# lora_A over ScalarE's queue in sixteen transfers instead of one over SyncE's

## The chip, the cores and the metric

The kernel runs on one core of one Trainium2 chip. The time is device microseconds of that core for one execution; the median of the runs is compared. The profile is of one execution, taken by the hardware profiler; its span runs from the first to the last instruction, and the execution's own time is somewhat longer than the span.

## The reference

A linear layer with a low-rank addition whose rank directions are scaled:

```
x_flat = x.reshape(-1, 256)                    # x: 16 x 2048 x 256, so 32768 rows
y = x_flat @ W                                 # W: 256 x 256
lora_out = ((x_flat @ lora_A) * lora_E) @ lora_B     # A: 256 x 16, E: 16, B: 16 x 256
out = y + scale * lora_out                     # scale = 1.0, all float32
```

## The kernel before

The kernel does not carry the low-rank path along with the data. It folds it into the weight once, at the start: weff = W + A diag(E) scale B, in bfloat16. Then each row of the output is one product of x with weff. To do this, PE transposes the two halves of lora_A (`a_sb`, L280) against an identity that POOL makes (L149 to L154), DVE scales the transposed A by `e_sb` into `ate` (L227), POOL casts `b_sb` to `b_bf` (L156), PE multiplies the two (L284), and DVE adds `w_sb` and writes `weff` (L233).

The 32768 rows are worked through in 32 steps of 8 x 128 rows. The transfers go in 11 chunks (`PLAN`), ten of three steps (3 MB each) and one of two (2 MB). SBUF has four buffers of three steps each, shared by inputs and outputs; `X_AT` and `Y_AT` say which chunk goes to which buffer. A chunk's load waits until every step of the chunk that used its buffer has been transposed (L128): loads 0 to 3 have a fresh buffer, load 4 waits for the six steps of chunks 0 and 1, load 5 for nine steps, and so on. All stores stand behind all loads on SyncE's queue, and the first store waits for the last load but one (L143).

A step goes through these stages. DVE rounds x to bfloat16 (`xb`, L198). PE transposes it as pairs of bfloat16 in float32 clothing into PSUM (`ps_xt`, L258). DVE or ACT copies that to `xt`, where up to 22 steps are kept (L188). DVE moves it to `xm` (L211). PE multiplies it by weff (L267) into `ps_y`, and ACT or DVE copies the result to the output buffer (L180). The order of DVE's work is written out by hand in `VECTOR`: r is a rounding, t a transposed step, m a move, y a result. In it, the making of `ate` and of `weff` stands right after `r0`, so that every later rounding stands behind it on DVE. The order on PE is set by `FIRST` and `SECOND`: the products of the first steps begin when six or seven rounds of transposes have been done, and the making of the low-rank product stands ahead of all transposes of x.

The transfers that concern the change are issued at L131 to L137, all by SyncE: W, chunk 0 of x, lora_A, lora_B, lora_E, then the other chunks. lora_A, lora_B and lora_E share the semaphore `s_l`, on which each adds 16, and three engines wait until it stands at 48 before they begin the low-rank path: POOL at L155, DVE at L225 and PE at L277.

ScalarE (ACT) issues no transfer. Its first instructions are the load of its activation table and then the copy of step 1's transposes (L188).

Of the kernel before, what the change touches and what calls it, by code (L numbers as in the profile page):

```python
# [20 lines left out]

FIRST = [6, 7, *range(14, 28)]
SECOND = [6, *range(13, 28)]


VECTOR = """
# [8 lines left out]
def kernel(  # L35
# [20 lines left out]
    KC = K // P  # L56
    H = S // Q
    CHUNKS, STEPS = len(PLAN), sum(PLAN)
    ROUNDS = max(*FIRST, *SECOND) + 1
    assert len(FIRST) + len(SECOND) == STEPS  # L60
    assert K == M == KC * P and STEPS * S * P == N

    def sbuf(name, shape, dt):
        return ctx.enter_context(nc.sbuf_tensor(name, shape, dt))
# [11 lines left out]
    a_sb = sbuf("a_sb", [P, KC, R], FP32)  # L76
# [15 lines left out]
    s_l = sem("s_l")  # L92
# [28 lines left out]
    with tc.tile_critical(sync_engine=mybir.EngineType.SP, no_gpsimd_drain=True):  # L121
        sp, pe, dve, act, pool = nc.sync, nc.tensor, nc.vector, nc.scalar, nc.gpsimd


        def load(i):
            if x_before[i] is not None:

                sp.wait_ge(s_t, first[x_before[i]] + PLAN[x_before[i]])  # L128
            sp.dma_start(out=rows_at(X_AT[i], 0, PLAN[i] * S), in_=rows_of(x_flat, i)).then_inc(s_io[i], 16)

        sp.dma_start(out=w_sb[:], in_=W.rearrange("(p c) m -> p c m", c=KC)).then_inc(s_w, 16)  # L131
        load(0)
        sp.dma_start(out=a_sb[:], in_=lora_A.rearrange("(p c) r -> p c r", c=KC)).then_inc(s_l, 16)
        sp.dma_start(out=b_sb[:], in_=lora_B).then_inc(s_l, 16)
        sp.dma_start(out=e_sb[:], in_=lora_E[:, None]).then_inc(s_l, 16)
        for i in range(1, CHUNKS):
# [8 lines left out]
        for i in range(CHUNKS - 3):  # L145
# [6 lines left out]
            out=ident[:], in_=ident[:], compare_op=mybir.AluOpType.not_equal, fill=1.0,  # L152
            base=0, pattern=[[-1, P]], channel_multiplier=1,
        ).then_inc(s_id, 1)  # L154
        pool.wait_ge(s_l, 48)  # L155
        pool.tensor_copy(out=b_bf[:], in_=b_sb[:]).then_inc(s_lora, 1)  # L156


# [15 lines left out]
        def y_of(q, engine, copy):  # L174
            k, h = q // H, q % H
            i = chunk[k]
            if y_before[i] is not None:
                ensure(engine, s_io[y_before[i]], 32)
            ensure(engine, s_p, q + 1)
            done = copy(out=rows_at(Y_AT[i], (k - first[i]) * S + h * Q, Q), in_=ps_y[h][:])  # L180
            last = k == first[i] + PLAN[i] - 1
            done.then_inc(s_rdy[h] if last else s_y[h], 1)

        def transposes_of(k, engine, copy):
            ensure(engine, s_t, k + 1)
            if k >= KEPT:
                ensure(engine, s_mv, k - KEPT + 1)
            copy(  # L188
                out=xt[:, k % KEPT].rearrange("w j p c -> w j (p c)"), in_=ps_xt[k % 2][:].bitcast(BF16),
            ).then_inc(s_c[k % 2], 1)  # L190


        def round_step(k):
            i = chunk[k]
            ensure(dve, s_io[i], 16)
            if k >= 2:
                ensure(dve, s_t, k - 1)
            dve.tensor_copy(  # L198
                out=xb[k % 2][:], in_=rows_at(X_AT[i], (k - first[i]) * S, S),
            ).then_inc(s_xb, 1)  # L200

        def move(k):


            if k + 2 < STEPS:
                ensure(dve, s_t, k + 3)
            else:
                dve.wait_ge(s_c[k % 2], 1)
            if k >= 2:
                ensure(dve, s_p, (k - 1) * H)  # L210
            dve.tensor_copy(out=xm[k % 2][:], in_=xt[:, k % KEPT]).then_inc(s_mv, 1)  # L211

        vectors = set(VECTOR.split())
        for what in VECTOR.split():
            n = int(what[1:])
            if what[0] == "r":
                round_step(n)
            elif what[0] == "t":
                transposes_of(n, dve, dve.tensor_copy)
            elif what[0] == "m":  # L220
                move(n)
            else:
                y_of(n, dve, dve.tensor_copy)
            if what == "r0":
                dve.wait_ge(s_l, 48)  # L225
                dve.wait_ge(s_lpe, 1)
                dve.tensor_scalar(  # L227
                    out=ate[:], in0=ps_at, scalar1=e_sb[:], scalar2=float(scale),
                    op0=mybir.AluOpType.mult, op1=mybir.AluOpType.mult,
                ).then_inc(s_lora, 1)  # L230
                dve.wait_ge(s_w, 16)
                dve.wait_ge(s_lpe, 2)
                dve.tensor_add(out=weff[:], in0=w_sb[:], in1=ps_aeb).then_inc(s_lora, 1)  # L233


        def rounds():
            k = 0
            for n in range(ROUNDS):
                for b, these in enumerate((FIRST, SECOND)):
                    if n in these:  # L240
# [33 lines left out]
            pe.sem_inc(s_y[h], 1)  # L274
        for b in range(2):
            pe.sem_inc(s_c[b], 1)
        pe.wait_ge(s_l, 48)  # L277
        pe.wait_ge(s_id, 2)
        for c in range(KC):
            t = pe.transpose(ps_at[:, c, :], a_sb[:, c, :], ident[:])  # L280
# [7 lines left out]

        bits = [sum(1 << n for n in these) for these in (FIRST, SECOND)]
        with pe.Fori(0, ROUNDS) as n:  # L290
# [45 lines left out]
```

## Time and profile before

| | |
|---|---|
| median of 2 runs | 166.51 us (166.48 to 166.55) |
| profiled execution | 166.21 us |
| its span | 164.4 us |
| busy, PE / DVE / ACT / POOL | 103.4 / 99.9 / 72.1 / 1.6 us |
| moved | 67.43 MB, mean 410 GB/s |
| issue to landing: W / lora_A / lora_B / lora_E | 2.7 / 9.4 / 9.2 / 9.4 us |
| mean granted clock of TensorE | 0.91 |

The page divides the span into 40 slices of some 4.1 us, with one digit of busy share each (9 is 90% or more). Engines are PE (TensorE), PEld (its weight loads), DVE (VectorE), ACT (ScalarE), POOL (GpSimd) and SP (SyncE); SPq is SyncE's own queue of transfers. q1 and q14 are queues of the sixteen DMA engines: q1 carries the kernel's transfers, q14 the fetching of instructions. A line of a timeline gives start, duration, engine, line of the code, operation, destination and source, and in brackets how long the engine had been idle and what ended that. A line of the waits gives who waited for whom, the sum, how often, and the longest.

### The profile page before, as it was taken

The numbers are of one execution on the slowest core, as the hardware profiler recorded it, in microseconds if no ns is written. First come the engines' busy times: TensorE is split into PE (matmuls) and PEld (weight loads), VectorE is DVE, ScalarE is ACT, GpSimd is POOL, SyncE is SP. The second block draws the span as 40 slices with busy tenths as digits, with TensorE's granted clock in tenths as the row PEclk, the third lists the DMA queues.
The fourth block names the chain that finished last, engine by engine and source line by source line (L and its number), as shares of the span: only waits on it lengthen the run. The fifth ranks groups of instructions, "written<-read, shape, count | busy, mean of one in ns | idle before, by whom it ended". The sixth has DMA issues, their size and how long they took to land. (4 is left out here: it accounts for less than half of the span.)

```text
span 164.4 us, 2431 instructions
## 1 busy us (share of the span) xinstructions
PE 103.4 (63%) x772; PEld 82.0 (50%) x772; DVE 99.9 (61%) x101; ACT 72.1 (44%) x62; POOL 1.6 (1%) x7
## 2 busy tenths in 40 slices
PE   0003763858884567966799887878878787880000
PEld 0001652747674447745699665655666565560000
DVE  0016699786969496787999765667466466730000
ACT  3000254146796413441477665446546544652000
POOL 1002000000000000000000000000000000000000
PEclk9999999599999675599999999999999999999555
DMA  5999999999999999999999999999999999999970
GB/s 165 460 403 460 401 460 401 460 401 460 401 466 395 466 395 466 395 466 385 420 460 401 454 407 460 413 442 424 436 424 436 424 432 424 442 424 430 426 301 12
DMA packets 3523, 67.43 MB, mean 410 GB/s; under 512 B 560, under 2 KB 576, under 8 KB 704
## 3 DMA queue, kind: packets, MB, share of 16 engines
q1 hardware_dynamic: 3520, 67.41, 96.2%
q14 instruction: 3, 0.02, 0.0%
HBM read 33.85 MB, written 33.55 MB: 410 GB/s over the span
## 5 line engine op out<-in xcount | busy, mean ns | idle before, releaser
L267 PE MATMUL ps_y<-weff,xm 128*128 128x256 bf16 x512 | 62.8, 272 | 9.9 <-PEq L264 8.8
L180 ACT COPY xy<-ps_y 128x1024 f32<-128x1024 f32 x49 | 48.7, 1016 | 35.2 <-PE ps_y L267 34.5
L267 PEld LDWEIGHTS ps_y<-weff,xm 128*128 128x128 bf16 x512 | 47.3, 97 | 24.3 <-issue 19.2
L258 PE MATMUL ps_xt<-ident,xb 128*128 128x128 f32 x256 | 41.4, 319 | 21.9 <-PEq L256 21.8
L198 DVE CAST xb<-xy 128x2048 bf16<-128x2048 f32 x32 | 38.6, 1221 | 23.7 <-DMA xy<-in_x_dram 20.2
L258 PEld LDWEIGHTS ps_xt<-ident,xb 128*128 128x128 f32 x256 | 34.7, 165 | 28.2 <-issue 28.1
L188 ACT COPY xt<-ps_xt 128x2048 bf16<-128x2048 bf16 x12 | 22.4, 1868 | 41.1 <-PE ps_xt L258 41.1
L180 DVE COPY xy<-ps_y 128x1024 f32<-128x1024 f32 x15 | 18.4, 1225 | 17.2 <-PE ps_y L267 17.2
L188 DVE COPY xt<-ps_xt 128x2048 bf16<-128x2048 bf16 x20 | 24.2, 1216 | 1.0 <-PE ps_xt L258 0.9
L211 DVE COPY xm<-xt 128x2048 bf16<-128x2048 bf16 x32 | 21.8, 685 | 4.4 <-PE ps_y L267 4.4
L280 PE MATMUL ps_y<-ident,a_sb 128*16 128x128 f32 x2 | 0.6, 402 | 12.2 <-DMA e_sb<-in_lora_E_dram 12.2
L280 PEld LDWEIGHTS ps_y<-ident,a_sb 128*16 128x16 f32 x2 | 0.1, 94 | 12.2 <-DMA e_sb<-in_lora_E_dram 12.2
L188 ACT ACT_TABLE_LOAD x1 | 1.3, 1283 | 0.9 <-SPq L121 0.9
L233 DVE TENSOR_TENSOR weff<-w_sb,ps_y 128x512 bf16<-128x512 f32 x1 | 0.7, 687 | 0.8 <-PE ps_y L284 0.8
L156 POOL CAST b_bf<-b_sb 16x256 bf16<-16x256 f32 x1 | 0.9, 912 | 10.6 <-DMA e_sb<-in_lora_E_dram 10.6
L284 PE MATMUL ps_y<-b_bf,ate 16*128 16x256 bf16 x2 | 0.6, 404 | 0.6 <-DVE ate L227 0.6
L284 PEld LDWEIGHTS ps_y<-b_bf,ate 16*128 16x128 bf16 x2 | 0.1, 106 | 1.1 <-DVE ate L227 1.1
L227 DVE TENSOR_SCALAR ate<-ps_y,e_sb 16x256 bf16<-16x256 f32 x1 | 0.5, 472 | 0.0
L151 POOL TENSOR_SCALAR_AFFINE_SELECT ident<-ident 128x128 f32<-128x128 f32 x1 | 0.3, 294 | 0.2 <-POOL ident L149 0.2
L149 POOL MEMSET ident<- 128x128 f32 x1 | 0.2, 205 | 0.5 <-SPq L121 0.5
L317 POOL MEMSET const-bfloat16-1.0<- 128x1 bf16 x1 | 0.1, 103 | 0.0
L317 POOL MEMSET const-uint8-127<- 128x1 uint8 x1 | 0.1, 102 | 0.0
(2 smaller groups left out, 0.2 us busy)
## 6 DMA issues: line engine op xcount, KB each, us to landing
xy<-in_x_dram SPq DMA_DIRECT2D x10, 3072.0 KB, 14.4
out_dram<-xy SPq DMA_DIRECT2D x10, 3072.0 KB, 12.5
xy<-in_x_dram SPq DMA_DIRECT2D x1, 2048.0 KB, 12.7
out_dram<-xy SPq DMA_DIRECT2D x1, 2048.0 KB, 13.7
w_sb<-in_W_dram SPq DMA_DIRECT2D x1, 256.0 KB, 2.7
a_sb<-in_lora_A_dram SPq DMA_DIRECT2D x1, 16.0 KB, 9.4
b_sb<-in_lora_B_dram SPq DMA_DIRECT2D x1, 16.0 KB, 9.2
e_sb<-in_lora_E_dram SPq DMA_DIRECT2D x1, 0.1 KB, 9.4
```

The source lines that it names most:

```text
L151: pool.affine_select(out=ident[:], in_=ident[:], compare_op=mybir.AluOpType.not_equal, fill=1.0, base=0, pattern=[[-1, P]], channel_multip ...
L156: pool.tensor_copy(out=b_bf[:], in_=b_sb[:]).then_inc(s_lora, 1)
L180: done = copy(out=rows_at(Y_AT[i], (k - first[i]) * S + h * Q, Q), in_=ps_y[h][:])
L188: copy(out=xt[:, k % KEPT].rearrange("w j p c -> w j (p c)"), in_=ps_xt[k % 2][:].bitcast(BF16),).then_inc(s_c[k % 2], 1)
L198: dve.tensor_copy(out=xb[k % 2][:], in_=rows_at(X_AT[i], (k - first[i]) * S, S),).then_inc(s_xb, 1)
L211: dve.tensor_copy(out=xm[k % 2][:], in_=xt[:, k % KEPT]).then_inc(s_mv, 1)
L227: dve.tensor_scalar(out=ate[:], in0=ps_at, scalar1=e_sb[:], scalar2=float(scale), op0=mybir.AluOpType.mult, op1=mybir.AluOpType.mult,).the ...
L233: dve.tensor_add(out=weff[:], in0=w_sb[:], in1=ps_aeb).then_inc(s_lora, 1)
L258: t = pe.transpose(ps_xt[b][:, j, :], xb[b][:, j, :].bitcast(FP32), ident[:])
L267: m = pe.matmul(ps_y[h][:, j, :], xm[b][:, h * Q + j, :, c], weff[:, c, :], start=(c == 0), stop=(c == KC - 1),)
L280: t = pe.transpose(ps_at[:, c, :], a_sb[:, c, :], ident[:])
L284: m = pe.matmul(ps_aeb[:, c, :], ate[:, c, :], b_bf[:], start=True, stop=True)
```

## The change

lora_A's 128 partitions are no longer loaded by one transfer of SyncE's queue that stands behind chunk 0, but by sixteen transfers that ScalarE issues, of 15, 14, 13 and so on down to 1 partitions and one of 8. They are ScalarE's first instructions, ahead of its table load. Each adds 16 to `s_l`, so the three waits ask for (16 + 2) x 16 = 288. The bytes moved are the same, and so are all other instructions and their order on each engine. In the diff, `p` runs over the partitions.

```diff
+A_PIECES = [*range(15, 0, -1), 8]
...
         load(0)
-        sp.dma_start(out=a_sb[:], in_=lora_A.rearrange("(p c) r -> p c r", c=KC)).then_inc(s_l, 16)
+
+        p = 0
+        for n in A_PIECES:
+            act.dma_start(
+                out=a_sb[p:p + n], in_=lora_A.rearrange("(p c) r -> p c r", c=KC)[p:p + n],
+            ).then_inc(s_l, 16)
+            p += n
         sp.dma_start(out=b_sb[:], in_=lora_B).then_inc(s_l, 16)
...
-        pool.wait_ge(s_l, 48)
+        pool.wait_ge(s_l, (len(A_PIECES) + 2) * 16)
...
-                dve.wait_ge(s_l, 48)
+                dve.wait_ge(s_l, (len(A_PIECES) + 2) * 16)
...
-        pe.wait_ge(s_l, 48)
+        pe.wait_ge(s_l, (len(A_PIECES) + 2) * 16)
```

## The prediction

> **What bounds the kernel now.** I read the page's slices and queues first, then the waits and SP's part of the timeline, then the first 16 us of the timeline, then the trace's own records of DMA packets (one for each packet, with start, duration and size).
>
> The transfers are the bound. In the slices, the DMA row stands at 9 from slice 1 to slice 37, and section 3 gives one queue 96.2% of sixteen engines' span; the stages say the same:
>
> ```profile
> DMA  5999999999999999999999999999999999999970
> q1 hardware_dynamic: 3520, 67.41, 96.2%
> ```
>
> ```profile
> 20.00:33.00 13.00, 7.71 (x48) 6.50 (x48) 11.94 (x12) 5.61 (x4) 0.00 (x0) 0.87 0.99 425
> 33.00:82.00 49.00, 34.73 (x240) 29.09 (x241) 39.05 (x37) 24.24 (x18) 0.00 (x0) 0.86 1.00 427
> 82.00:150.00 68.00, 56.50 (x466) 43.11 (x464) 43.38 (x49) 40.34 (x41) 0.00 (x0) 1.00 1.01 432
> ```
>
> (Columns: stretch, length, busy PE, PEld, DVE, ACT, POOL, granted clock, DMA share, GB/s.) The reader is to see a DMA share of 0.99 to 1.01 in every stage, with DVE at 80% or less after 33 us. So a change costs time only where it makes the sixteen engines idle or gives one of them more work, and gains only by the opposite.
>
> The second thing to read is where they could be made idle. Loads 4 to 10 reuse buffers and wait for transposes:
>
> ```profile
> SPq L140 <- ACT xy L180: 67.7, 10, 8.0
> SPq L129 <- PE ps_xt L258: 63.4, 7, 21.7
> SPq L331 <- DMA out_dram<-xy: 12.5, 1, 12.5
> ```
>
> The longest of the seven waits, 21.7 us, is that of load 4, which waits for six steps of transposes; three lines of the timeline show how they come to start:
>
> ```profile
> 2.80 0.55 SPq L135 DMA_DIRECT2D e_sb<-in_lora_E_dram  x1
> 3.39 1.42 SPq L129 DMA_DIRECT2D xy<-in_x_dram  x3
> 11.68 1.23 DVE L198 CAST xb<-xy 128x2048 bf16<-128x2048 f32 x1 [11.68 <-DMA xy<-in_x_dram]
> 12.23 0.60 PE L280 MATMUL ps_y<-ident,a_sb 128*16 128x128 f32 x2 [12.23 <-DMA e_sb<-in_lora_E_dram]
> ...
> 14.79 1.22 DVE L198 CAST xb<-xy 128x2048 bf16<-128x2048 f32 x1
> ```
>
> ```profile
> 26.54 0.33 SPq L129 DMA_DIRECT2D xy<-in_x_dram  x1
> ```
>
> PE, DVE and POOL all stand at the low-rank semaphore until 12.19 us, when the last increment of e_sb lands. I call that moment L. Load 4 is issued at 26.54, so 14.35 us after L, and the work between (rounding, transposes, evictions) waits for no load. Loads 0 to 3 keep the engines busy meanwhile: chunk 3's increments land from 32.98 to 33.71, and a last packet ends some 0.3 us before its increment, so the engines run dry at about 32.8. A load's first packet starts 1.0 us after its issue (W: issued at 0.95, first packet at 1.96). Load 4 may therefore be issued as late as 31.8, and L may slip from 12.2 to about 17.5 us before one engine idles. Past that, each microsecond of L is a microsecond of the run: all that follows is transfers end to end.
>
> **The change, part by part.** *SP gives up one issue* (0.42 us and a gap of 0.04): b_sb, e_sb and loads 1 to 3 are issued 0.46 us sooner. That gains nothing, as they stand behind chunk 0 on the engines: e_sb, issued at 2.80, landed at 12.19. The 128 packets of a_sb leave that queue: 8 a engine of 13 ns and one semaphore packet of 9 ns, 0.11 us. If e_sb still ended the wait, L would be 12.1: hidden under the 5.3 us of slack.
>
> *ACT gets sixteen issues.* No row shows ACT issuing; SP's take 0.33 to 0.55 us, so 5.3 to 8.8 us, and I take 0.45 with the gap, 7.2 us: from 0.95 (where the table load starts now) to 8.1, then the table load, 1.28 us, to 9.4. Cover: ACT's first copy starts at 19.41 after 17.2 us of idleness. Even 1 us an issue would be hidden; without the cover each would delay that copy by itself.
>
> *The three waits* ask for 288 instead of 48; they wait for the same data. Behind them stand, on PE every transpose, on DVE every rounding after the first, on POOL the cast of b_sb and the passing on of semaphores. If the pieces are late, all of it is.
>
> *Packets.* The data are the same 128 packets of 128 bytes. Before, each of 26 transfers put 16 semaphore packets of 4 bytes on the engines (432 such records, 16 of them e_sb's data). A piece of n partitions has at most n shares: 128 semaphore packets against 16. The busiest engine gets at least 8 data packets (an even spread) and at most one from each piece if every transfer starts over at the same engine, 16. No row shows which. Nearest is that in all later stores one and the same engine falls further behind (last landing 0.5 us behind the next in the fourth store, 2.4 us in the last), as if every transfer was cut over the engines alike; so I take 16. The Trainium skill (DMA: Bandwidth & Descriptors, "Why a DMA increments its semaphore by 16 and not by 1") says that such a transfer uses the largest count up to 16 that divides both sides, on the lowest-numbered engines; by that it is 16 too, and no row here can show it. As plain work the busiest engine's share is 16 x (13 + 9) ns instead of 113 ns: 0.24 us more, hidden unless it is the engine that ends the stores, 2.4 us behind the others. Ends: 0 and 0.24; I take 0.
>
> *The two queues.* This is the large term, and in the trace of before q1 carries everything of the kernel. The nearest rows are three foreign packets on q14 (8192 bytes, at 77.02, 134.13 and 154.74). The first two start the moment a packet of the stream ends on one engine and take 333 and 309 ns, and that engine's next packet starts when they are done (77.34, 134.43): one packet at a time, the newcomer in after a single packet of chunk 10. So a queue's turn seems to last one packet. By the time the stream starts (first packets of chunk 0 at 2.84 to 3.45), pieces issued 0.45 us apart and 1.0 us under way have had 3 through; 13 are left. If the queues alternate, each packet of a piece waits for one of the stream, 0.912 us (median of 2560). Per piece the ends are: nothing (the newcomer is always let in, L stays 12.1), one stream packet (0.912, data and semaphore in one turn: L = 3 + 11.9 = 14.9), two (1.82, a turn each). I take two, since both are records of their own: L = 3 + 13 x 1.82 = 26.7, with 0.3 to land 27.0.
>
> **Sum.** Load 4 at 27.0 + 14.35 = 41.35, its first packet at 42.35; engines dry from 32.8: 9.5 us of idle. Load 5 followed load 4 by 7.76 us (34.30 less 26.54) and is needed after 7.3 + 0.25 us of packets, so 0.2 more, and later ones catch up: load 6 came 5.5 us after. Between 9.0 (the last engine dry at 33.4) and 9.7; I take 9.5. The profiled execution took 166.21 us (1.8 outside its span), 0.3 under the median of the runs: 166.2 + 9.5 = 175.7.
>
> **The rivals.**
>
> *No change: the pieces are let in.* One mechanism decides, the price of a piece on the busiest engine. L stays under 17.5 as long as it is at most 1.1 us, and the time moves by 2% (3.3 us) from 1.37 us on. For it: the q14 packets were let in at once, and one turn would do for data and semaphore; an even spread (8 pieces on an engine, some 6 of them late) gives L = 3 + 6 x 1.82 = 14 and ends the same. Against: all four chunks stand in the queue by 4.8 us, so the stream never pauses. Time 166.2 to 166.4.
>
> *The return to the stream costs.* After the packet at 77.02, the stream's next took 1273 ns instead of 611, and that chunk's landings spread over 1.20 us instead of 0.72; in the two stores the loss was 116 and 88 ns. If each piece costs its engine 0.912 + 0.66, L = 3 + 13 x 1.57 = 23.4, and that engine lies 13 x 0.66 = 8.6 us behind with its own loads, which every chunk and the stores' start wait for: 174.8. With two such returns a piece, 26 x 1.57 = 41, L = 44, load 4 at 58.3; the engine has then 17.2 us of its own delay and 9 of idle: about 191.
>
> *A turn lasts a whole transfer.* Then a piece waits for 8 packets, 7.3 us, and most are stuck until the stream runs dry: L about 33.8, load 4 at 48.1, idle from 32.8 to 49.1: 182.5. The q14 packet that came in after one packet of a chunk speaks against it. The Trainium skill (same page, "Queues, rings and completion order") speaks for it: an engine goes round the queues and drains a whole packet, typically 9 to 17 descriptors, before it switches. By that rule it would be this rival.
>
> **How the numbers follow.** Two turns a piece: 0.38, its own range 172.5 to 178. No change: 0.36 (let in 0.14, one turn 0.15, even spread 0.07). One return a piece: 0.13. Whole transfers: 0.06. Two returns: 0.05. Faster: 0.02, as nothing takes work from the engines that end the run. The likeliest is two turns, 175.7. The range takes in no change at its low end and whole transfers at its high end, 165.9 to 183.0, and leaves out the two returns. Slower by over 2% (about what a measurement of this kernel can tell from no change): 0.38 + 0.13 + 0.06 + 0.05 = 0.62; same 0.36; faster 0.02.
>
> **What would show it.** Right: PE's first transpose (a_sb) near 27 us instead of 12.23, released by a_sb's transfer; load 4 near 41; slices 8 to 10 of the DMA row falling; a second queue with 256 packets. ACT's issues end by 9 us and its first copy waits for PE. Wrong: a_sb landed before 17.5 us and the DMA row unbroken (no change); or stream packets longer than 0.92 us on one engine while the pieces last (returns); or landings of pieces 7.3 us apart (whole transfers).

## The result and the profile after

The changed kernel takes 177.81 us (median of two runs, 177.74 and 177.87) against 166.51 us: a ratio of 1.068, 95% interval 1.063 to 1.072. The forecast was 175.7 us, slower, by a start of PE at about 27 us and idle transfer engines until load 4. Both are there; the time is 2.1 us above the forecast. Two of the runs below had one execution in a slower state of the chip, which is left out of their medians and ratios.

The profiled execution took 177.87 us with a span of 176.1 us. These are the page's rows of the changed kernel that answer to those shown of before:

```profile
DMA  5999999303899999999999999999999999999980
q1 hardware_dynamic: 3376, 67.39, 90.1%
q10 hardware_dynamic: 256, 0.02, 0.1%
```

The unbroken row of nines has a hole, slices 7 to 10, and a second queue, q10, carries 256 packets: 128 of data and 128 of the semaphore. The same hole by stages (stretch, length, busy PE, PEld, DVE, ACT, POOL, granted clock, DMA share, GB/s):

```profile
20.00:33.00 13.00, 4.46 (x20) 3.50 (x20) 3.58 (x5) 0.00 (x0) 0.39 (x1) 1.00 0.96 412
33.00:43.00 10.00, 7.68 (x34) 6.55 (x32) 9.01 (x9) 4.34 (x3) 0.00 (x0) 1.00 0.00 0
43.00:82.00 39.00, 25.21 (x192) 21.26 (x192) 32.72 (x31) 23.27 (x16) 0.00 (x0) 0.96 1.00 423
```

For ten microseconds nothing was moved. The timeline of the changed kernel says how that came about:

```profile
0.91 6.12 ACTq L138 DMA_DIRECT2D a_sb<-in_lora_A_dram  x16
...
25.91 0.59 PE L288 MATMUL ps_y<-ident,a_sb 128*16 128x128 f32 x2 [25.91 <-DMA a_sb<-in_lora_A_dram]
...
28.47 1.22 DVE L206 CAST xb<-xy 128x2048 bf16<-128x2048 f32 x1
29.74 3.65 PE L266 MATMUL ps_xt<-ident,xb 128*128 128x128 f32 x16 [1.99 <-DVE xb L206]
...
34.22 3.65 PE L266 MATMUL ps_xt<-ident,xb 128*128 128x128 f32 x16 [0.84 <-PEq L264]
...
38.71 3.65 PE L266 MATMUL ps_xt<-ident,xb 128*128 128x128 f32 x16 [0.83 <-PEq L264]
```

```profile
42.38 0.33 SPq L131 DMA_DIRECT2D xy<-in_x_dram  x1
```

ScalarE has issued its sixteen pieces by 7.03 us, and yet PE waits for the last of them until 25.91. Load 4 follows at 42.38 us instead of 26.54. SP's waits show the same as a sum, the longest of the seven (load 4's) having grown from 21.7 to 38.1 us:

```profile
SPq L131 <- PE ps_xt L266: 73.9, 7, 38.1
```

Where the pieces were, the trace's packet records show. These are the last ones of the changed kernel, with the stream packets that stand between them (start in us, duration in ns, bytes, queue):

```
22.69   13    128  q10
22.70  912  24576  q1
23.61    9      4  q10
...
24.52   13    128  q10
24.53  912  24576  q1
25.44    9      4  q10
```

A data packet of 128 bytes, one stream packet of 0.912 us, its semaphore packet, one more stream packet, the next data packet: a piece takes two turns, 1.83 us, though its own packets last 22 ns. The last packet is at 25.44 us and its increment is counted at 25.87.

The end moved as the hole did. Chunk 4's last increment came 18.75 us behind chunk 3's (52.39 and 33.64 us) instead of 7.30, 11.45 us more; the next loads each came 7.3 us after the one ahead of it, and the last store landed at 174.65 us instead of 162.99, 11.66 later.

### The profile page after: what moved, and what is told of

Read it like the earlier page. It is cut to its first block, busy times and chain, and to the rows that moved or that the text cites. A ratio compares the mean times of both kernels' runs of the same rounds, so it can differ in the third digit from the quotient of the medians.

```text
span 176.1 us, 2446 instructions
## 1 busy us (share of the span) xinstructions
PE 102.7 (58%) x772; PEld 82.2 (47%) x772; DVE 99.8 (57%) x101; ACT 72.0 (41%) x62; POOL 1.1 (1%) x7
## 5 line engine op out<-in xcount | busy, mean ns | idle before, releaser
L188 ACT COPY xy<-ps_y 128x1024 f32<-128x1024 f32 x49 | 48.8, 1017 | 35.7 <-PE ps_y L275 35.1
L275 PEld LDWEIGHTS ps_y<-weff,xm 128*128 128x128 bf16 x512 | 47.2, 97 | 24.6 <-issue 19.5
L266 PE MATMUL ps_xt<-ident,xb 128*128 128x128 f32 x256 | 40.6, 318 | 20.2 <-PEq L264 18.2
L206 DVE CAST xb<-xy 128x2048 bf16<-128x2048 f32 x32 | 38.7, 1223 | 22.2 <-DMA xy<-in_x_dram 17.2
L188 DVE COPY xy<-ps_y 128x1024 f32<-128x1024 f32 x15 | 18.4, 1225 | 17.2 <-PE ps_y L275 17.2
L288 PE MATMUL ps_y<-ident,a_sb 128*16 128x128 f32 x2 | 0.6, 398 | 25.9 <-DMA a_sb<-in_lora_A_dram 25.9
L288 PEld LDWEIGHTS ps_y<-ident,a_sb 128*16 128x16 f32 x2 | 0.1, 92 | 25.9 <-DMA a_sb<-in_lora_A_dram 25.9
L164 POOL CAST b_bf<-b_sb 16x256 bf16<-16x256 f32 x1 | 0.4, 388 | 24.2 <-DMA a_sb<-in_lora_A_dram 24.2
```

The source lines that it names most:

```text
L206: dve.tensor_copy(out=xb[k % 2][:], in_=rows_at(X_AT[i], (k - first[i]) * S, S),).then_inc(s_xb, 1)
L266: t = pe.transpose(ps_xt[b][:, j, :], xb[b][:, j, :].bitcast(FP32), ident[:])
L275: m = pe.matmul(ps_y[h][:, j, :], xm[b][:, h * Q + j, :, c], weff[:, c, :], start=(c == 0), stop=(c == KC - 1),)
```

## The experiments

The theory: the packets of a second queue take turns with those of the stream, one packet a turn, on the engine at which every piece starts; so the low-rank data come late, load 4 with them, and the engines run dry. The rivals: that sixteen small transfers are dear in themselves, that a second queue is, or that a turn lasts a whole transfer. In all of them L is the moment at which the low-rank data are complete, read from PE's first transpose, which starts some 0.04 us later. Ratios are to the kernel before on the same chip.

**The same pieces on one queue.**

```diff
-            act.dma_start(
+            sp.dma_start(
```

> The same sixteen pieces, issued by SyncE on the stream's own queue. Theory (two queues take turns, so that both packets of a piece wait for one stream packet of 0.912 us each on the engine where all pieces start): on one queue nothing alternates, the pieces pass in a row behind chunk 0, the low-rank data are complete at 11.5 to 12.5 us; chunk 1 is issued 7 us later, at about 9.8, just as the engines run dry, which may cost 0 to 1 us: 166.3 to 167.5 us. Rival (sixteen small transfers with their 128 semaphore packets are dear on any queue): complete after 20 us, 170 us or more.

Measured: 167.89 us, ratio 1.009 (1.008 to 1.011); L at 14.44. So all but 1.5 of the 11.3 us go when only the queue is changed, and sixteen transfers are not what costs most. But the loss is 1.5 us where 0 to 1 was expected. Chunk 1 was issued at 8.43, early enough. The pieces' packets had all started by 11.62 us, but the stream's packets behind them took up to 2.49 us instead of 0.912: over chunk 1, from 10.7 to 20.5 us, 15.1 us more in all on the sixteen engines, against 0.1 us in before. Chunk 1's landings came from 18.77 to 20.89 us instead of 18.38 to 19.10; taken in order, each of the sixteen is 0.3 to 1.8 us later, and a spread of 2.1 us or more stayed for the later loads. Why the packets behind are longer, the records do not show.

**An even spread over the engines.**

```diff
-A_PIECES = [*range(15, 0, -1), 8]
+A_PIECES = [16] * 8
```

> Eight pieces of 16 partitions over ScalarE's queue: the same 256 packets, but each engine gets 8 data and 8 semaphore packets. Theory: two pieces pass before the stream, some at the boundary behind chunk 0, the others cost 1.82 us each: complete at 12 to 14.5 us, under the 17.5 us from which the engines idle: 166.3 to 166.8 us. Rival (the second queue or the number of packets in all costs, not the busiest engine): complete at 20 us or later, 172 us or more.

Measured: 166.41 us, ratio 1.001 (1.000 to 1.002). It is as the theory says; the same number of packets on the same second queue costs nothing when no engine has more than eight pieces:

```profile
12.90 0.60 PE L288 MATMUL ps_y<-ident,a_sb 128*16 128x128 f32 x2 [12.90 <-DMA a_sb<-in_lora_A_dram]
```

**Which engines.**

```diff
-A_PIECES = [*range(15, 0, -1), 8]
+A_PIECES = [8] * 16
```

> Sixteen pieces of 8 partitions over ScalarE's queue, 256 packets again. If every transfer starts over at the same engine, eight engines get 16 pieces each: complete at 24 to 27 us, 176 to 179 us, as with the uneven pieces. If pieces are spread over the engines in rotation, each engine gets 8: complete at 12 to 14.5 us, 166.3 to 166.8 us.

Measured: 177.56 us (176.31 to 178.66), ratio 1.070 (1.066 to 1.073):

```profile
26.03 0.59 PE L288 MATMUL ps_y<-ident,a_sb 128*16 128x128 f32 x2 [26.03 <-DMA a_sb<-in_lora_A_dram]
```

The last eight semaphore packets come together, from 24.69 to 25.51 us, as they must if all sixteen pieces went to the same eight engines. The prediction's 16 on the busiest engine is thereby shown by rows. That agrees with the section of the Trainium skill that it named; that these are the lowest-numbered engines, no run shows.

**How long a turn is.** One transfer of all of lora_A on ScalarE's queue, issued once the stream runs:

```diff
-A_PIECES = [*range(15, 0, -1), 8]
+A_PIECES = [128]
...
+        act.wait_ge(s_w, 16)
         p = 0
```

> One transfer of all 128 partitions over ScalarE's queue, issued only when W has landed (about 3.8 us), so that the stream is under way. Turn of one packet: the 8 data packets and the semaphore packet of an engine come 0.912 us apart, but for those that pass at the boundary behind chunk 0; complete at 11.5 to 13.5 us. Turn of a whole transfer: an engine's 8 packets come in a row within 0.2 us. Time 166.3 to 166.8 us by both; the packet records tell them apart.

Measured: 166.26 us, ratio 0.9995 (0.9985 to 1.0005), L at 12.53. One engine's first data packets start at 7.50, 8.42, 9.34 and 10.26 us, 0.92 apart, each with a stream packet behind it, and the rest pass behind chunk 0, where the stream has small packets of its own. A turn is one packet even within one transfer. The rule of the Trainium skill (DMA: Bandwidth & Descriptors, "Queues, rings and completion order"), that an engine drains a packet of typically 9 to 17 descriptors before it switches, does not hold for these two queues. What stays open is why the first of these packets came 3.7 us after the issue (3.79 us), where the changed kernel's first piece took 1.0 (0.91 to 1.94).

**The price of a turn is the stream's packet.** Each load of x is cut into one transfer a step, so that its packets hold 8192 bytes; in the waits, the counts grow with the number of transfers. Once with the change and once without:

```diff
-            sp.dma_start(out=rows_at(X_AT[i], 0, PLAN[i] * S), in_=rows_of(x_flat, i)).then_inc(s_io[i], 16)
+            for r in range(PLAN[i]):
+                sp.dma_start(
+                    out=rows_at(X_AT[i], r * S, S), in_=rows_of(x_flat, i)[:, r * S:(r + 1) * S, :],
+                ).then_inc(s_io[i], 16)
```

> The changed kernel, but each load of x is cut into one transfer for each step, so that the stream's packets hold 8192 bytes instead of 24576 (about 0.31 us instead of 0.912). Theory (a packet of a piece waits for one packet of the stream): a piece costs 0.62 us instead of 1.82, the low-rank data are complete at 11 to 13 us, no engine idles for them: 166 to 168 us, as the uncut kernel before. Rival (a piece has a price of its own, 1.8 us, from its semaphore or from the change of queues): complete near 26 us and about 177 us as before the cut.

> The kernel before with the same cut, as the measure for the changed kernel with the cut: low-rank data complete near 12.2 us; 166 to 168 us, if three times as many load packets cost no more than their semaphores. The changed kernel with the cut should lie within 0.5 us of it.

Measured: 168.05 us with the change (ratio 1.011, 1.009 to 1.013) and 168.18 without it (1.012, 1.010 to 1.013). With the change:

```profile
13.04 0.60 PE L291 MATMUL ps_y<-ident,a_sb 128*16 128x128 f32 x2 [13.04 <-DMA a_sb<-in_lora_A_dram]
```

The sixteen pieces, their engine and their queue are as in the changed kernel; only the packets that they wait for are a third as long, and L falls from 25.9 to 13.0 us and the whole loss with it. (The cut itself costs 1.7 to 1.9 us, in both.)

**Late data without a second queue.** lora_A in one transfer of SyncE, moved behind chunk 1 (the edit shown) and behind chunk 2 (the same with `i == 2`):

```diff
-        sp.dma_start(out=a_sb[:], in_=lora_A.rearrange("(p c) r -> p c r", c=KC)).then_inc(s_l, 16)
...
         for i in range(1, CHUNKS):
             load(i)
+            if i == 1:
+                sp.dma_start(out=a_sb[:], in_=lora_A.rearrange("(p c) r -> p c r", c=KC)).then_inc(s_l, 16)
```

> lora_A in one transfer on SyncE's queue as before, but behind chunk 1 instead of chunk 0: no second queue, only late data, complete at 19.3 to 19.7 us. Theory (the lateness alone costs, through load 4): load 4 is issued 14.35 us (as before) to 16.5 us (as in the changed kernel) later, at 33.7 to 36.2, and the engines idle 2 to 5 us: 168.5 to 171.5 us. Rival (the loss comes from the second queue, lateness matters little): 166.5 us.

> lora_A in one transfer on SyncE's queue behind chunk 2: complete at 26.6 to 27.0 us, about 1 us later than in the changed kernel, with no second queue. Theory: load 4 at 41 to 43.5, idle for 9.9 to 12.3 us: 176.1 to 178.7 us, as long as the changed kernel. Rival (most of the loss comes from the second queue): under 170 us.

Measured: 170.28 us (ratio 1.025, 1.021 to 1.030) with L at 19.46, and 178.44 us (1.068, 1.062 to 1.074) with L at 26.56. The second has one queue and one transfer, and its DMA row has the hole of the changed kernel:

```profile
DMA  6999999201999999999999999999999999999980
q1 hardware_dynamic: 3520, 67.41, 90.0%
```

So lateness alone makes the whole loss, and the first run puts its beginning where the slack of the prediction ended: at L = 19.5, 2 us past the 17.5 foretold, it costs 4.1 us.

**Data as early as can be.**

```diff
-        sp.dma_start(out=a_sb[:], in_=lora_A.rearrange("(p c) r -> p c r", c=KC)).then_inc(s_l, 16)
-        sp.dma_start(out=b_sb[:], in_=lora_B).then_inc(s_l, 16)
-        sp.dma_start(out=e_sb[:], in_=lora_E[:, None]).then_inc(s_l, 16)
+        act.dma_start(out=a_sb[:], in_=lora_A.rearrange("(p c) r -> p c r", c=KC)).then_inc(s_l, 16)
+        act.dma_start(out=b_sb[:], in_=lora_B).then_inc(s_l, 16)
+        act.dma_start(out=e_sb[:], in_=lora_E[:, None]).then_inc(s_l, 16)
```

> lora_A, lora_B and lora_E in one transfer each over ScalarE's queue, issued first of all, so that they are ahead of the stream. Theory (only idle transfer engines cost time): complete at 3.5 to 5 us, the low-rank product made right after the first rounding, load 4 up to 1 us sooner, the time as before, 166.0 to 166.5 us. Rival (the start of the low-rank product counts by itself): 165.5 us or less.

Measured: 166.30 us, ratio 1.000 (0.999 to 1.001). L was 7.96, later than expected: issued at 0.90 to 2.26 us, part of the packets met the stream. Load 4 came 0.21 us sooner (26.33), and the time is that of before. Starting earlier buys nothing; no version here beats the kernel before.

**Why load 4 came later than foretold.** In the changed kernel it followed L by 16.5 us, not 14.35. Its first three pairs of steps take 3.65 us for 16 transposes, 228 ns each, where most pairs of before take 132. The profile's PEclk row shows 9 there, but the trace's first clock record (to full) is at 42.54 us, 18.89 in before, so the row has nothing to go by ahead of it. The Trainium skill (TensorE: Matmul & The Clock Gate, "Part 1: The HAM clock gate") says that TensorE runs at half rate after idleness and that busyness is judged in free-running windows of 3413 ns; the records here do lie multiples of 3.41 us apart. To try it, PE was kept busy ahead of the wait:

```diff
+        pe.wait_ge(s_id, 2)
+        for _ in range(160):
+            pe.transpose(ps_xt[0][:, 0, :], ident[:], ident[:])
         pe.wait_ge(s_l, (len(A_PIECES) + 2) * 16)
-        pe.wait_ge(s_id, 2)
```

> The changed kernel with 160 extra transposes of the identity on PE ahead of the wait (their results are overwritten), so that PE is busy until about 25 us. Theory (the 2.1 us that load 4 came later than forecast after the low-rank data are TensorE's slow first 12.8 us, 228 ns a transpose against 132): data complete at 25.9 as before, transposes of steps 0 to 5 at 132 ns, load 4 at 38.9 to 40.3, 174.3 to 175.7 us. Rival (the clock does not matter, something else delays load 4): 177.8 us, or more if the extra work is in the way.

Measured: 177.30 us (176.39 to 178.64), ratio 1.069 (1.064 to 1.075). It did not settle it: the extra work ended at 21.1 us, 4.8 before the data, and a clock record shows half speed from 25.7. In the profiled execution one pair was slow instead of three, and load 4 came at 40.20. The same on the kernel before, with 55 transposes:

> The kernel before with 55 extra transposes of the identity on PE ahead of the wait. Load 4 should be issued about 1 us sooner (the first pair of steps at 132 ns a transpose), which is hidden, since the engines have loads until 32.8 us: 166.3 to 166.7 us by the theory that only idle transfer engines cost time. Rival (PE's start counts by itself): 165.5 us or less.

Measured: 166.24 us, ratio 1.001 (0.999 to 1.002). The expected microsecond did not come: the extra work ended 2.35 us ahead of the data, a clock record shows half speed from 12.23 us, and the first pair was slow again (3.52 us). Load 4 was issued at 26.27, 0.3 us sooner, and no time was gained with it, so this run says little. In the next attempt, 200 transposes ahead of the wait and 5 and 16 in the two gaps behind it (`busy(n)` issues n transposes of the identity):

```diff
+        pe.wait_ge(s_id, 2)
+        busy(200)
         pe.wait_ge(s_l, (len(A_PIECES) + 2) * 16)
...
+        busy(5)
         pe.wait_ge(s_lora, 2)
...
+        busy(16)
         pe.wait_ge(s_lora, 3)
```

> The changed kernel with 200 extra transposes of the identity on PE ahead of the wait and 21 more in the gaps of the low-rank product (results overwritten), so that PE has no gap over about 1 us from 2 us on. Theory (the slow transposes of steps 0 to 5 are TensorE's clock after idleness): data complete at 25.9, all steps at 132 ns a transpose, load 4 at 39 to 40.3 us instead of 42.38, 174.8 to 176.4 us in every run, without the spread of the first attempt. Rival (the slow transposes do not come from idleness): load 4 near 42.4, 177.8 us.

Measured: 176.00 us (174.99 to 177.55), ratio 1.057 (1.053 to 1.060). No step of the first six is slow any more, and load 4 came at 40.12, 13.2 us after L (which was 26.9 instead of 25.9; why, the record does not show). But the times spread all the same, and the profiled execution was the longest of the four, 177.55 us. Its timeline shows where the gain went:

```profile
26.91 0.39 PE L293 MATMUL ps_y<-ident,a_sb 128*16 128x128 f32 x2 [0.29 <-DMA a_sb<-in_lora_A_dram]
...
30.48 2.07 PE L266 MATMUL ps_xt<-ident,xb 128*128 128x128 f32 x16 [0.25 <-PEq L264]
34.09 1.06 PE L266 MATMUL ps_xt<-ident,xb 128*128 128x128 f32 x8 [1.54 <-PEq L264]
...
42.45 3.65 PE L266 MATMUL ps_xt<-ident,xb 128*128 128x128 f32 x16 [2.35 <-PEq L264]
```

At 41.71 the granted clock was halved, steps 6 and 7 ran at 228 ns a transpose, and load 5, which waits for step 8, came 8.78 us after load 4 instead of 5.78. The theory stands for load 4; that the run would be short and even was wrong. The profiled executions side by side (us):

| kernel | L | load 4 | load 4 less L | slow pairs of the first three | load 5 less load 4 | time |
|---|---|---|---|---|---|---|
| before | 12.2 | 26.54 | 14.3 | 1 | 7.76 | 166.21 |
| pieces, 16 each | 12.9 | 28.07 | 15.2 | 2 | 7.96 | 166.25 |
| one late transfer | 12.5 | 29.00 | 16.5 | 3 | 5.78 | 166.54 |
| behind chunk 1 | 19.5 | 34.64 | 15.2 | 2 | 7.57 | 170.28 |
| pieces, 8 each | 26.0 | 40.33 | 14.3 | 1 | 8.04 | 176.31 |
| change, PE busy once | 25.9 | 40.20 | 14.3 | 1 | 7.81 | 176.39 |
| change, PE busy all along | 26.9 | 40.12 | 13.2 | 0 | 8.78 | 177.55 |
| change | 25.9 | 42.38 | 16.5 | 3 | 5.78 | 177.87 |
| behind chunk 2 | 26.6 | 43.00 | 16.4 | 3 | 5.82 | 178.44 |

The way from L to load 4 takes 13.2, 14.3, 15.2 or 16.5 us as none, one, two or three pairs are slow, in all nine.

Why one execution gets one slow pair and another three, the clock records show. Laid back from the first record in steps of 3.41 us, the changed kernel's windows that end at 32.3, 35.7 and 39.1 us have PE busy for 75 to 76% and leave the slow pace; the one that ends at 42.54 has it busy for 94% and ends it. In before, the window that ends at 18.89 is 83% busy and ends it at once. A pair of steps is 3.65 us of work and 0.84 us of idleness; a window that holds the whole of that gap is 75% busy, one that cuts it is busier. The same working for all fourteen profiled executions (their first 150 us) agrees: each of the 60 changes to full clock follows a window that is at least 80% busy, none of the 113 windows that leave the clock at half is above 84%, each of the 46 changes to half clock follows a window below 48%, and none of the 383 that leave it full is below 47%. (The pace ahead of the first record is taken as the slow one.) What decides between 80 and 84% is open. This was worked out from the traces afterwards; no run was made to test it.

In both busy versions one engine lay a further microsecond behind in chunk 1 (landings over 1.54 and 1.69 us instead of 0.72). Their pages have a queue that the changed kernel's does not, a second one for the fetching of instructions:

```profile
q8 instruction: 2, 0.03, 0.1%
```

Its packets hold 16384 bytes. One of 0.92 us stands at 14.48 us in the first busy version and one of 1.03 us at 16.26 in the second, among the packets of one engine while chunk 1 was on its way. In the kernel before with 55 transposes the only one is at 20.22 us, and there it is chunk 2 whose landings spread (2.07 us; chunk 1's 0.58). No run without extra transposes has one. So the extra instructions themselves cost a transfer engine about a packet of the stream.

## Why the prediction was right, and where its sizes were off

- *The bound and the slack.* Right. The engines run dry at 32.6 to 33.2 us (last packets of chunk 3), foretold for 32.8 to 33.4; no hole opens while L is under 17.5 (12.9, 13.0 and 14.4 us), and at 19.5 one does.
- *Two turns a piece.* Right, by the records: 1.83 us against 1.82. Sixteen pieces on one engine was right too.
- *L.* 25.9 against 27.0, two errors that partly cancel, which is luck. Only two pieces were through before the stream's first packets, not three (the third starts at 4.16, behind a first stream packet). And behind chunk 0, where lora_B's and lora_E's small packets are the stream's, about two pieces passed without waiting for long packets (the 27 intervals between the 28 packets of the other fourteen pieces, from 4.16 to 25.44 us, take 21.3 us instead of 27 x 0.912 = 24.6); the sum had left that out.
- *From L to load 4.* 16.5 against 14.35: the mis-sized term. It was taken from before as work that waits for no load, which is so, but before had one slow pair of transposes and the changed kernel three, 2.1 us. How many an execution gets hangs on where the clock's windows lie, so a part of the 2.1 us above the forecast is chance: the pieces of 8 partitions, with one slow pair and nearly the same L (26.0), took 176.31 us in the profiled execution.
- *The hole.* From 42.38, the first packets started 0.96 us after the issue, as taken (1.0), but thirteen of chunk 4's first sixteen took 1.41 us or more instead of 0.912, so that the stream needed about 0.6 us to be back; the sum had none of that for load 4. And load 5, for which 0.2 us more was set aside, came 5.78 us after load 4 and cost nothing. Together chunk 4 was 11.45 us late, against 9.5 in the sum: 1.0 of the difference is load 4's issue (42.38 against 41.35), 0.6 the slow first packets; the rest is not accounted for.
- *ACT's issues.* 6.12 us against 7.2, hidden as said: the table load began at 7.06, and the first copy waited 25.1 us for PE.
- *The rivals.* No change fell because a piece cost 1.83 us, above the 1.37 from which it was to show; it came true where the price fell (8192-byte packets) or the number did (an even spread). The return to the stream cost nothing: between 13 and 31 us all but one of the stream's 317 packets took 912 to 926 ns, and that one 951. (The terms given for two returns a piece, 166.2 + 17.2 + 9, add up to 192.4, not 191; nothing hangs on it.) A turn as long as a transfer fell by the records of the one late transfer.
- *Small packets as work.* 0.24 us was the end of that range, at nothing in the sum. Between long packets it was nothing (chunk 1's landings spread over 0.66 us); in a row it made landings up to 1.8 us later (the pieces on one queue).
- *The range.* 165.9 to 183.0 took in no change as well as whole transfers, so a time inside it says little by itself. What bears the forecast out is its mechanism, to which it gave 0.38: the two turns of 0.912 us a piece, the sixteen pieces on one engine, and the hole until load 4.

## What to carry to other kernels

A small transfer on a second queue does not slip past a stream: on each engine it pays one of the stream's packets for each of its own, the semaphore's included, so count its packets on the busiest engine and multiply by the stream's packet. Cut a small load so that every engine gets an equal share, issue it ahead of the stream, or shorten the stream's packets if it must go beside it. And work out the slack of a start-up step from the first transfer that waits for it, with the chip's slow pace after idleness in the sum.

## What the runs showed of the hardware that was not expected

- On one queue, the 128 pairs of small packets in a row made chunk 1's packets behind them 15.1 us longer in all on the sixteen engines, about 0.12 us a pair (an estimate from these rows), where the records give a pair 22 ns; between stream packets they cost nothing that the landings show.
- TensorE needed from 29.74 to 42.54 us to leave its slow pace although it was busy for 3.65 of each 4.49 us; in before, one such stretch, 16.07 to 19.38, was enough. In windows of 3.41 us, 75 to 76% busy was too little, over 84% was always enough, and between 80 and 84% both happened.
- 55 to 221 more transposes on PE brought one or two fetches of 16384 bytes on a queue of their own, each of 0.92 to 1.03 us on one transfer engine.
